# A transformer block on one core: the first projection pass also takes the values' products of four token tiles

## The chip, the core and the metric

The kernel runs on one core of one Trainium2 chip. The metric is the device time of one execution in microseconds, as the median of several runs of the same program. Lower is better.

## The reference, cut to what matters

The kernel computes one block: a gated delta-rule branch (GDN, 4 heads of 128) and a dilated attention branch (8 heads of 64) over the same normed input, an output projection, and a gated feed-forward part, all in float32.

```python
def reference(x, w_in, conv_w, a_log, dt_bias, onorm_g, rel_bias, w_out, g_mix_pre, g_mix_post,
              w_gate, w_up, w_down, g_ffn_pre, g_ffn_post):
    split_at = [int(c) for c in np.cumsum(IN_SIZES)[:-1]]
    for l in range(DEPTH):
        h = rmsnorm(x, g_mix_pre[l])
        proj = h @ w_in[l]
        qa, ka, va, gate_a, beta_a, alpha_a, qb, kb, vb = jnp.split(proj, split_at, axis=-1)
        out_a = gated_deltanet(qa, ka, va, gate_a, beta_a, alpha_a,
                               conv_w[l], a_log[l], dt_bias[l], onorm_g[l])
        out_b = dilated_attention(qb, kb, vb, rel_bias)
        mix = jnp.concatenate([out_a, out_b], axis=-1) @ w_out[l]
        x = x + rmsnorm(mix, g_mix_post[l])
        h = rmsnorm(x, g_ffn_pre[l])
        f = (jax.nn.silu(h @ w_gate[l]) * (h @ w_up[l])) @ w_down[l]
        x = x + rmsnorm(f, g_ffn_post[l])
    return x
```

x is 1024 tokens by 1024 features. Only the start matters here: `h @ w_in`. The row factor of the norm (1 over the root mean square of a token) is put on after the product, so the products can start on x times g alone.

## The kernel before, in words

**Precision.** A float32 product is made of three fp32r products: the left side is split into hi and lo, the right side too, and hi x hi, hi x lo and lo x hi are added in PSUM (`mm3`, line 555). A split takes one instruction on ACT (or DVE) for hi, a cast, and one on DVE (or POOL) for lo.

**Input.** x comes transposed in tiles of one k tile (128 features) by half of the tokens (512): `load_xt` (line 1302) issues the load of `xT`, 256 KB, and `prep_xt` makes `hTh` on ACT and `hTl` on DVE. There are 16 such tiles, eight for each half; six xT buffers. x comes a second time in token tiles (`load_x`, line 1316, 512 KB, three buffers `xn`), from which `norm_in` takes the row factor: a square with a running sum on ACT into `junk`, two small operations on DVE and POOL, `rtok`; for each four tiles four transposes on PE turn it into `rb`, the factor along the tokens.

**Weights.** Chunks of 128 columns of w_in come in two pieces of four k tiles each (`wr`, 256 KB, four buffers). `prep_w` (line 697) splits a piece and fires an event for it.

**The first items.** ORDER (line 57) begins with k0, q0, bv0: GDN's first key and query head, then the first half of the attention values with the eight columns of beta and alpha (264 columns in all, chunks 24 and 25, `wba`). `main` (line 1252) runs, for each half of the tokens, `proj_first` (line 723), which takes k0 and q0 side by side into two PSUM banks `pj` (48 products of 512 columns, a k tile at a time), and then `proj_v` for four token tiles (line 770; 24 products of 264 columns for each tile, into a bank `tp`). I call the two runs of `proj_first` the first and the second pass. There are two `pj` banks and four `tp` banks. A `pj` bank of these passes is emptied by a copy to `raw` on ACT (`raw_sink`, line 1223), which is multiplied by `rb` later; a `tp` bank by two ACT instructions, `vs` (the values, stored to `d_v` by a DMA of 128 KB) and `bp` (beta and alpha).

**What sets the order.** All instructions are issued by a planner (`Weaver`, line 237). Work is written as strands that yield an instruction, a request for a buffer or an event; the planner keeps a clock for each engine, takes the instruction that by its own costs can start first, and among those by priority. So the order on each engine is fixed when the program is built, and each engine runs its instructions in that order. DMAs of this part are issued from SP's queue, also in order; a DMA's issue can wait for a buffer. A request for a buffer is granted when the planner reaches it, without an instruction: who asks first has it.

Of the kernel before, what the change touches and what calls it, by code (L numbers as in the profile page):

```python
# [48 lines left out]
LATE = 2000.0  # L49
PB = 2  # L50
SW = 832

FAR = {2: 256, 3: 576, 4: 448, 5: 416, 6: 256, 7: 576}
PWO = (2, 3, 2)
# [158 lines left out]
class After:  # L213


    def __init__(self, *aps, late=0.0):
        self.aps, self.late = aps, late


class Strand:  # L220
# [16 lines left out]
class Weaver:  # L237
# [125 lines left out]
    def run(self, *until):  # L363
        while not all(e.set for e in until):
# [15 lines left out]
            for s in live:  # L380
                if s.alts is not None:
                    s.req = s.alts[0]
                    if s.ver >= 0:
                        s.req = min(s.alts, key=lambda r: self.finish(s, r, live))
                names = [x.tensor.name for x in s.req.aps] if isinstance(s.req, After) else \
                    [x[0] for op in s.req for x in op.ins + op.outs]
                v = sum(self.ver.get(n, 0) for n in names)
                if v != s.ver:
                    s.ver = v
                    if isinstance(s.req, After):  # L390
                        s.data = max([t for x in s.req.aps for t, _ in self.wr.get(x.tensor.name, {}).values()] + [0.0])
# [12 lines left out]
                first = min(first, s.start)  # L404
# [137 lines left out]
def block_kernel(ctx: ExitStack, tc: tile.TileContext, a, out):  # L542
# [109 lines left out]

    def load_w():

        first = chunks(order[0]) + chunks(order[1])
        got = {c: [] for c in first}
        evs = {c: [Event() for _ in range(2)] for c in first}
        for i in range(2):
            for n, c in enumerate(first):
                wr = yield rawS.get([P, 4, P], F32, name="wr")  # L660
                yield SY.dma_start(wr[:], a["w_in"][c][:, 4 * i:4 * i + 4, :])
                got[c].append(wr)
                evs[c][i].fire()
                if not i:
                    w.spawn(prep_w(c, got[c], evs[c]), 1)
                yield from load_xt(4 * i + n, 0)
                if not i and not n:
                    yield SY.dma_start(gT[:], a["g_mix_pre_t"])
            for k in (2, 3):
                yield from load_xt(4 * i + k, 0)  # L670
        yield SY.dma_start(wba[:], a["w_ba"])
        yield from load_item(order[2])
        yield SY.dma_start(ident[:], a["c_ident"])
        for t in range(4):
            yield from load_x(t)
        for k in range(KT):
            yield from load_xt(k, 1)
        for t in range(4, NT):
            yield from load_x(t)
        ev_x.fire()  # L680
        for item in order[3:]:
            yield from load_item(item)

    def load_item(item):
        for c in chunks(item):
            z, evs = [], [Event() for _ in range(2)]
            for i in range(2):
                wr = yield rawS.get([P, 4, P], F32, name="wr")
                yield SY.dma_start(wr[:], a["w_in"][c][:, 4 * i:4 * i + 4, :])
                z.append(wr)  # L690
                evs[i].fire()
            w.spawn(prep_w(c, z, evs), 1)

    ev_x = Event()
    ev_wh = {(c, i): Event() for c in loaded for i in range(2)}

    def prep_w(c, raw, got):
        hi, lo = [], []
        for i in range(4):
            if c in (24, 25):  # L700
                z = yield wS.get([P, 2, WB], F32R, name="w")
            else:
                z = yield wS.get([P, 4, P], F32R, name="w")
            (lo if i % 2 else hi).append(z)
        wts[c] = hi, lo
        for i, (wh, wl) in enumerate(zip(hi, lo)):
            yield got[i]
# [9 lines left out]
            yield After(wr[:])  # L717
            yield from split_sb(wh, wl, wx)
            rawS.put(wr)
            ev_wh[c, i].fire()  # L720
# [33 lines left out]
    def proj_qk(c0, m, ev):  # L754
# [12 lines left out]
        for hf in range(2):  # L767
            yield from proj_half(c0 + m, hf, sink)

    def proj_v(m, tiles=range(NT)):  # L770
        c0 = 24 + 2 * m
        yield loaded[c0]
        yield loaded[c0 + 1]
        wc = [wts[c0], wts[c0 + 1]]
        n = 256 if m else WB

        def sink(t, ps, bank):
            vs = yield outS.get([P, 4, 64], F32, name="vs")
            yield ev_r[t]
            r = rtok[:, t:t + 1]  # L780
            yield A.activation(vs[:], ps[:, 0:256].rearrange("p (h d) -> p h d", h=4), AF.Copy, scale=r)
            if not m:
                yield A.activation(bp[:, :, t], ps[:, 256:WB], AF.Copy, scale=r)
            (pj if m else pt).put(bank)
            yield SY.dma_start(d_v[t, :, 4 * m:4 * m + 4, :], vs[:])
            outS.put(vs)
            ev_v[m][t].fire()
        for t in tiles:
            if m:
                bank = ps = yield pj.get([P, n], F32, name="pj")  # L790
            else:
                bank = yield pt.get([P, 4, P], F32, name="tp")
                ps = bank[:].rearrange("p k j -> p (k j)")[:, 0:n]
            for k0 in range(0, KT, 2):
                ops = []
                wh, wl = (z[k0 % 4 // 2] for z in wc[k0 // 4])
                for k in (k0, k0 + 1):
                    h, l = (z[:, k % 2, :] if not m else z[:].rearrange("p (k x) c -> p k (x c)", x=2)[:, k % 2, :]
                            for z in (wh, wl))
                    ops += mm3(ps[:], *h_of(k, t * P, P), h, l, k == 0, k == KT - 1)  # L800
                yield ops
                if t == NT - 1:
                    wS.put(wh, wl)
            w.spawn(sink(t, ps, bank), 1)
        if not m and tiles[-1] == NT - 1:
            w.spawn(beta_alpha(ev_v[0]), 2)

# [444 lines left out]
    def main():  # L1252
# [43 lines left out]
    with ExitStack() as s0:  # L1296
# [10 lines left out]
        def prep_xt(k, hf, x):  # L1307
# [5 lines left out]
            px.put(x)  # L1313
            ev_xt[k, hf].fire()

        def load_x(t):
            x = yield px.get([P, D], F32, name="xn", bufs=3)
            yield SY.dma_start(x[:], a["x"][t * P:(t + 1) * P, :])
            done_in.append(w.spawn(norm_in(t, x), 1))

        def norm_in(t, x):
            ss = px.tile([P, 1], F32, name="ss%d" % t)
# [6 lines left out]
            if t % 4 == 3:  # L1329
# [1131 lines left out]
```

## Time and profile before

| | us |
|---|---|
| median of 3 runs | 1217.29 |
| the runs | 1215.97 to 1217.84 |
| the profiled execution's own time | 1217.08 |
| its span, first to last instruction | 1215.3 |
| mean granted TensorE clock | 0.998 of full speed |
| first product on PE starts at | 5.08 |
| second pass starts at | 30.70 |

All times in a profile are counted from the span's start. PE is TensorE's products, PEld its weight loads, DVE VectorE, ACT ScalarE, POOL GpSimd, SP the queue that issues DMAs. The length that the profile gives a product is longer than the distance to the next one, since products overlap in the array; rates are read from starts. Instructions are named out<-in with the kernel's tile names; all of them have the line of the planner's issue, so the names tell them apart.

### The profile page before, as it was taken

The page shows a single profiled execution, that of the slowest core. Times are in us where ns is not written, and L with a number is a line of the kernel's source. Part 1 is how long each engine was busy: PE and PEld are TensorE (multiplying, and loading weights), DVE is VectorE, ACT ScalarE, POOL GpSimd, SP SyncE. Part 2 cuts the span into 40 slices and gives each one's busy share as a digit, 9 for nine tenths or more (in the row PEclk, how much of TensorE's full clock was granted, in tenths as well). Part 3 has the DMA queues.
Part 4 walks back from the last instruction along what each step waited for, and adds up shares of the span by engine and source line. Part 5 has one row for each costly group of instructions (what it writes and reads, how often), then busy time and mean ns, then how long its engine had stood idle before and what let it go on. Part 6 is the DMA issues. An engine that isn't in the chain of part 4 may idle for free.

```text
span 1215.3 us, 19597 instructions
## 1 busy us (share of the span) xinstructions
PE 1198.3 (99%) x7135; PEld 996.0 (82%) x7135; DVE 886.0 (73%) x1633; ACT 544.8 (45%) x1060; POOL 158.0 (13%) x138
## 2 busy tenths in 40 slices
PE   8999999999999999999999999999999999999997
PEld 7888798788888778888788888888888887888886
DVE  4689969646665756676998876787667867876886
ACT  7645622226665654464643333333333344544541
POOL 0143311001111100011101110011100100000111
PEclk9999999999999999999999999999999999999999
DMA  8655363677546355774444433432233238644335
GB/s 279 197 154 164 104 188 102 135 236 239 195 143 204 112 170 181 234 242 163 133 156 139 131 121 122 130 110 70 90 121 122 82 122 312 223 138 149 102 122 207
DMA packets 152359, 192.76 MB, mean 159 GB/s; under 512 B 29976, under 2 KB 77848, under 8 KB 152264
## 3 DMA queue, kind: packets, MB, share of 16 engines
q1 hardware_dynamic: 148040, 189.43, 48.5%
q10 hardware_dynamic: 4224, 2.10, 0.6%
q8 instruction: 56, 0.92, 0.3%
q14 instruction: 39, 0.32, 0.1%
HBM read 135.62 MB, written 59.66 MB: 161 GB/s over the span
## 4 chain that ended last, share of the span: by engine, by line
PE 90%; DVE 4%; DMA 2%; issue 1%; ACT 1%; POOL 1%; SPq 0%; DVEq 0%; POOLq 0%; ACTq 0%
PE bank L286 48%; PE pj L286 22%; PE pw L286 6%; PE tp L286 5%; PE p L286 3%; PE pS L286 2%; PE pV L286 2%; PE pm L286 2%; DVE yc L286 1%; DMA views<-in_w_down 1%; DMA mx<-d_mix 0%; SPq L286 0%; DMA db<-in_w_down 0%; DMA cbv<-d_bv 0%; DVE x L286 0%
## 5 line engine op out<-in xcount | busy, mean ns | idle before, releaser
L286 PE MATMUL pj<-hTh,w 128*128 128x512 f32 x768 | 263.5, 404 | 5.1 <-ACT hTh L286 5.1
L286 PEld LDWEIGHTS pj<-hTh,w 128*128 128x128 f32 x768 | 145.2, 189 | 39.4 <-issue 5.3
L286 ACT CAST wbh<-wraw 128x512 fp32r<-128x512 f32 x130 | 80.4, 621 | 198.6 <-PE bank L286 122.1
L286 PE MATMUL pj<-hTl,w 128*128 128x512 f32 x384 | 151.0, 393 | 0.0
L286 DVE TENSOR_TENSOR wbl<-wraw,wbh 128x512 fp32r<-128x512 f32 x131 | 92.3, 707 | 29.1 <-ACT wbh L286 29.0
L286 PE MATMUL bank<-views 128*128 128x512 f32 (+1 forms) x307 | 85.0, 385 | 0.2 <-ACT views L286 0.2
L286 PEld LDWEIGHTS pj<-hTl,w 128*128 128x128 f32 x384 | 72.9, 190 | 12.5 <-DVE hTl L286 0.7
L286 PE MATMUL bank<-views,dah 128*128 128x512 f32 (+1 forms) x214 | 73.5, 379 | 0.0
L286 PE MATMUL bank<-dbh,views 128*128 128x512 f32 (+1 forms) x201 | 70.3, 380 | 0.0
L286 PEld LDWEIGHTS bank<-views 128*128 128x128 f32 x307 | 57.4, 188 | 12.0 <-ACT views L286 0.7
L286 POOL TENSOR_TENSOR m<-m,m 128x512 f32<-128x512 f32 x18 | 28.0, 1556 | 253.3 <-DVE r L286 153.3
L286 ACT CAST w<-wr 128x512 fp32r<-128x512 f32 x53 | 32.6, 618 | 50.5 <-PE pj L286 43.3
L286 PE MATMUL bank<-dbh,dah 128*128 128x512 f32 (+1 forms) x129 | 49.1, 381 | 0.0
L286 DVE TENSOR_TENSOR w<-wr,w 128x512 fp32r<-128x512 f32 x44 | 30.7, 703 | 23.2 <-ACT w L286 22.0
L286 DVE SCALAR_TENSOR_TENSOR yc<-raw,convw,yc 128x1024 f32<-128x1024 f32 x36 | 46.6, 1294 | 0.5
L286 PEld LDWEIGHTS bank<-views,dah 128*128 128x128 f32 x214 | 40.0, 188 | 7.7
L286 PE MATMUL pw<-woh,mh 128*128 128x512 f32 x112 | 45.2, 404 | 0.0
L286 PE MATMUL pw<-woh,ml 128*128 128x512 f32 x112 | 43.8, 391 | 0.0
L286 PE MATMUL pw<-wol,mh 128*128 128x512 f32 x112 | 43.7, 390 | 0.0
L286 PEld LDWEIGHTS bank<-dbh,views 128*128 128x128 f32 x201 | 37.7, 188 | 7.1
L286 DVE TENSOR_TENSOR m<-bank,m 128x512 f32<-128x512 f32 x44 | 30.1, 686 | 18.1 <-PE bank L286 18.0
L286 ACT ACTIVATE Sr<-Sr,mx 128x384 f32<-128x384 f32 (+3 forms) x64 | 38.2, 597 | 6.4 <-DVE mx L286 5.9
(384 smaller groups left out, 3073.8 us busy)
## 6 DMA issues: line engine op xcount, KB each, us to landing
wr<-in_w_in SPq DMA_DIRECT2D x56, 256.0 KB
wraw<-in_w_gate SPq DMA_DIRECT2D x52, 256.0 KB
wraw<-in_w_up SPq DMA_DIRECT2D x52, 256.0 KB
views<-d_hid SPq DMA_DIRECT2D x47, 256.0 KB
db<-in_w_down SPq DMA_DIRECT2D x40, 256.0 KB
da<-d_hid SPq DMA_DIRECT2D x30, 256.0 KB
d_hid<-x SPq DMA_DIRECT2D x22, 256.0 KB
d_hid<-r SPq DMA_DIRECT2D x22, 256.0 KB
```

The lines of the kernel that those rows point to most:

```text
L286: op.fn(*op.args, **op.kw)
```

## The change

The first pass also takes the values' products of the first four token tiles, two k tiles at a time: after each two k tiles of k0 and q0 stand 24 products of the values into four `tp` banks. The weights of k0 and q0 are loaded and split in pieces of two k tiles (128 KB), with an event for each; the value weights' pieces stand between them on SP's queue, and `gT` and `wba` come early. `After` can wait for a part of a tile. A new strand, `warm`, sets 512 columns of `junk` to zero and then yields ten bf16 products on them in a `tp` bank. The strands of `norm_in` get a slack of SPREAD = 5000: their transposes are held back on PE until their data are 5 us old by the planner's clock, unless nothing else can go. The sink of the values and the list of their products become functions of their own, `v_sink` and `v_ops`.

```diff
     def load_w():
+        yield SY.dma_start(gT[:], a["g_mix_pre_t"])
...
+        for k in range(0, KT, 2):
+            i, j = k // 4, k % 4
             for n, c in enumerate(first):
...
+                yield SY.dma_start(got[c][i][:, j:j + 2, :], a["w_in"][c][:, k:k + 2, :])
+                evs[c][i][j // 2].fire()
...
+                yield from load_xt(k + n, 0)
+            if not k:
+                yield SY.dma_start(wba[:], a["w_ba"])
+            c = vs[i]
+            wr = yield rawS.get([P, 4, P], F32, name="wr")
...
+            yield SY.dma_start(wr[:], a["w_in"][c][:, 2 * j:2 * j + 4, :])
...
     def proj_first(hf, sinks):
...
+        vs = []
+        if not hf:
+            for t in range(4):
+                z = yield pt.get([P, 4, P], F32, name="tp")
+                vs.append(z)
         for k in range(KT):
             for c, z in zip(cs, ps):
-                yield ev_wh[c, k // 4]
+                yield ev_wh[c, k // 2]
...
+            if vs and k % 2:
+                yield ev_wh[24 + k // 4, k % 4 - 1]
+                for t, z in enumerate(vs):
+                    yield v_ops(0, t, v_rows(0, z), k - 1)
+        for t, z in enumerate(vs):
+            w.spawn(v_sink(0, t, v_rows(0, z), z), 1)
...
-            yield from proj_v(0, range(4 * hf, 4 * hf + 4))
+        yield from proj_v(0, range(4, NT))
...
+        def warm():
+            yield V.memset(junk[:, 0:512], 0.0)
+            tp = yield pt.get([P, 4, P], F32, name="tp")
+            yield [mm(tp[:].rearrange("p k j -> p (k j)"), junk[:, 0:P], junk[:, 0:512]) for _ in range(10)]
+            pt.put(tp)
...
-            done_in.append(w.spawn(norm_in(t, x), 1))
+            done_in.append(w.spawn(norm_in(t, x), 1, SPREAD))
...
+        w.spawn(warm(), 0)
```

What the planner makes of it is seen in the order of the built programs, without times. On PE before, at the program's start, with buffer numbers (pj_157 is k0's bank, pj_158 q0's; w_162 and w_173 their hi weights):

```order
L2457 UNCONDITIONAL_BRANCH
L286 MATMUL pj_157<-hTh_104,w_162 128x512
L286 MATMUL pj_157<-hTl_105,w_162 128x512
L286 MATMUL pj_157<-hTh_104,w_163 128x512
L286 MATMUL pj_158<-hTh_104,w_173 128x512
L286 MATMUL pj_158<-hTl_105,w_173 128x512
L286 MATMUL pj_158<-hTh_104,w_174 128x512
```

On PE now, from the ninth product of the program (pj_156 and pj_157 are the two banks, tp_158 the first value tile's, w_187 and w_188 hi and lo of the values' first piece):

```order
L287 MATMUL pj_156<-hTh_104,w_171 128x512
L287 MATMUL pj_157<-hTh_104,w_178 128x512
L287 MATMUL pj_157<-hTl_105,w_178 128x512
L287 MATMUL pj_157<-hTh_104,w_179 128x512
L287 MATMUL tp_158<-w_187,hTh_104 128x264
L287 MATMUL tp_158<-w_188,hTh_104 128x264
L287 MATMUL tp_158<-w_187,hTl_105 128x264
```

The first twelve products are those of before, and behind them stand value products instead of the next k tile. On PE now, where the first pass with its values ends and the second pass begins:

```order
L287 MATMUL tp<-w,hTl 128x264
L287 LDWEIGHTS junk
L287 MATMUL tp<-junk 128x512
...
L287 MATMUL tp<-ident,rtok 128x128 x4
L287 MATMUL pj<-hTh,w 128x512
L287 MATMUL pj<-hTl,w 128x512
```

The ten products on `junk` stand here, each with a weight load, and nowhere else: at the program's start `proj_first` asks for all four `tp` banks before `warm`'s memset is issued. On ACT before, around the copies of the first pass:

```order
L286 CAST w<-wba 128x2x8
L286 COPY raw<-pj 128x512
L286 CAST w<-wr 128x2x256
L286 COPY raw<-pj 128x512
L286 ACTIVATE junk,ss_268<-xn 128x1024
L286 ACTIVATE junk,ss_274<-xn 128x1024
L286 ACTIVATE vs<-tp,rtok 128x256
```

On ACT now, up to the same two copies; four squares into `junk` and four `hTh` of the second half and the first `vs` stand ahead of these rows:

```order
L287 ACTIVATE hTh<-xT,gT 128x512
L287 ACTIVATE bp<-tp,rtok 128x8
L287 ACTIVATE hTh<-xT,gT 128x512
L287 ACTIVATE vs<-tp,rtok 128x256
L287 ACTIVATE hTh<-xT,gT 128x512
L287 ACTIVATE bp<-tp,rtok 128x8
L287 ACTIVATE hTh<-xT,gT 128x512
L287 ACTIVATE vs<-tp,rtok 128x256
L287 ACTIVATE bp<-tp,rtok 128x8
L287 ACTIVATE vs<-tp,rtok 128x256
L287 ACTIVATE bp<-tp,rtok 128x8
L287 COPY raw<-pj 128x512 x2
```

The copies to `raw` have moved from ahead of the evictions of the value tiles, and ahead of the second half's `hTh`, to behind them all. On SP the eight `xT` loads of the second half now follow each other, with the four `d_v` stores behind them; before, two stores stood among them. From the second pass on the order on PE is that of before, apart from buffer numbers.

More of the change, by code (lines that the diff above doesn't have):

```diff
@@ L213, with __init__ @@
 class After:
-    def __init__(self, *aps, late=0.0):
-        self.aps, self.late = aps, late
+    def __init__(self, *aps, late=0.0, part=False):
+        self.aps, self.late, self.part = aps, late, part
 class Strand:
@@ L390, in run @@
                     if isinstance(s.req, After):
-                        s.data = max([t for x in s.req.aps for t, _ in self.wr.get(x.tensor.name, {}).values()] + [0.0])
+                        own = [self.region(x) if s.req.part else (x.tensor.name, -1, -1) for x in s.req.aps]
+                        s.data = max([t for n, q, f in own for (p, g), (t, _) in self.wr.get(n, {}).items() if p & q and f & g] + [0.0])
                     else:
@@ L685, in load_item @@
         for c in chunks(item):
-            z, evs = [], [Event() for _ in range(2)]
+            z, evs = [], [[Event()] for _ in range(2)]
             for i in range(2):
@@ L716, in prep_w @@
                 wh, wl, wx = wh[:], wl[:], wr[:]
-            yield After(wr[:])
-            yield from split_sb(wh, wl, wx)
+            for j, ev in enumerate(got[i]):
+                yield ev
+                x = (slice(None), slice(2 * j, 2 * j + 2) if len(got[i]) > 1 else slice(None))
+                yield After(wx[x], part=len(got[i]) > 1)
+                yield from split_sb(wh[x], wl[x], wx[x])
+                ev_wh[c, 2 * i + j].fire()
             rawS.put(wr)
-            ev_wh[c, i].fire()
         loaded[c].fire()
@@ L768, in proj_qk, with v_rows, v_ops, v_sink @@
             yield from proj_half(c0 + m, hf, sink)
+    def v_rows(m, bank):
+        return bank if m else bank[:].rearrange("p k j -> p (k j)")[:, 0:WB]
+    def v_ops(m, t, ps, k0):
+        c0 = 24 + 2 * m
+        ops = []
+        wh, wl = (z[k0 % 4 // 2] for z in wts[c0 + k0 // 4])
+        for k in (k0, k0 + 1):
+            h, l = (z[:, k % 2, :] if not m else z[:].rearrange("p (k x) c -> p k (x c)", x=2)[:, k % 2, :]
+                    for z in (wh, wl))
+            ops += mm3(ps[:], *h_of(k, t * P, P), h, l, k == 0, k == KT - 1)
+        return ops
+    def v_sink(m, t, ps, bank):
+        vs = yield outS.get([P, 4, 64], F32, name="vs")
+        yield ev_r[t]
+        r = rtok[:, t:t + 1]
+        yield A.activation(vs[:], ps[:, 0:256].rearrange("p (h d) -> p h d", h=4), AF.Copy, scale=r)
+        if not m:
+            yield A.activation(bp[:, :, t], ps[:, 256:WB], AF.Copy, scale=r)
+        (pj if m else pt).put(bank)
+        yield SY.dma_start(d_v[t, :, 4 * m:4 * m + 4, :], vs[:])
+        outS.put(vs)
+        ev_v[m][t].fire()
     def proj_v(m, tiles=range(NT)):
```

64 lines of the change are left out of this document (22 added, 42 removed).

## The prediction

> **What bounds the kernel now.** The page comes first: how full TensorE (PE) is, and how much of the chain that ended last runs on it.
>
> ```profile
> span 1215.3 us, 19597 instructions
> PE 1198.3 (99%) x7135; PEld 996.0 (82%) x7135; DVE 886.0 (73%) x1633; ACT 544.8 (45%) x1060; POOL 158.0 (13%) x138
> PE 90%; DVE 4%; DMA 2%; issue 1%; ACT 1%; POOL 1%; SPq 0%; DVEq 0%; POOLq 0%; ACTq 0%
> ```
>
> PE is busy for 99% of the span and carries 90% of the chain. So a change pays or costs what it takes out of, or puts into, PE's own row of work. Next the chain in order of time (start, length, what), for the first part of the program, which is all that the change touches, and where this stretch of PE pieces ends.
>
> ```profile
> 5.08 13.68 PE pj L286 x48
> 18.77 12.09 PE tp L286 x100
> 30.86 10.89 PE pj L286 x48
> 41.75 12.08 PE tp L286 x100
> 53.83 5.45 PE pj L286 x24
> ...
> 117.45 4.80 PE pj L286 x21
> ```
>
> From 5.08 us on PE pieces follow each other: the first pass (48 products into two pj banks), four token tiles of the values (96 products and four transposes, tp), the second pass, the other four tiles. Between 53.83 and 122.25 (117.45 + 4.80) the chain stays on PE too. So if the second pass starts later by some amount, all that follows starts later by that amount. Where it starts is the whole question. Now PE's timeline at those places (start, length, what, how many; in brackets the idle time before and what ended it):
>
> ```profile
> 5.08 0.79 PE L286 MATMUL pj<-hTh,w 128*128 128x512 f32 x1 [5.08 <-ACT hTh L286]
> 8.75 0.63 PE L286 MATMUL pj<-hTl,w 128*128 128x512 f32 x1
> 9.18 0.97 PE L286 MATMUL pj<-hTh,w 128*128 128x512 f32 x2
> 9.99 0.39 PE L286 MATMUL pj<-hTl,w 128*128 128x512 f32 x1
> ...
> 18.60 0.41 PE L286 MATMUL tp<-w,hTh 128*128 128x264 f32 x2
> ...
> 28.07 0.60 PE L286 MATMUL tp<-ident,rtok 128*128 128x128 f32 x4
> 28.43 0.49 PE L286 MATMUL tp<-w,hTh 128*128 128x264 f32 x2
> ...
> 30.70 0.39 PE L286 MATMUL pj<-hTh,w 128*128 128x512 f32 x1
> ```
>
> Starts count here, not lengths. At 8.75 a product follows its neighbour after 0.43 us: the clock is still low. From 9.99 to 18.60 stand the last 38 of the 48, 0.227 us each. The first ten took 4.91 us, of which 10 x 0.427 = 4.27 is the low clock and 0.64 is waiting for h and weights. The four transposes take 0.36 (28.07 to 28.43), so the 96 value products take 30.70 - 18.60 - 0.36 = 11.74, or 0.122 each.
>
> **The change part by part.** *The products themselves.* The same 48 and 96 products run, two k tiles of the weights and then two of the values in turn. PE starts when the first h tile is ready, as before. Ten of the twelve products of the first pair lie in the low clock again, for the zeros are not ahead of them: in the built order they stand behind the last value product (the last order rows under the change). So the end of this block, T1, is 30.70 - 0.36 = 30.34. Smaller pieces can at best remove the 0.64 of waiting; at worst the first value piece is late. I bound that by the longest wait of PE in the trace, 1.3:
>
> ```profile
> PE tp L286 <- DVE y L286: 1.6, 2, 1.3
> ```
>
> I take 0 within -0.6 and +1.0, for after the first pair data lead. A pair keeps PE for 24 x 0.122 + 12 x 0.227 = 5.7 us, and in five such us the DMA moves more than the 1 MB that a pair needs (two xT of 256 KB, two half and one whole piece of weights); one stage's row, with DVE's busy time as its third count and GB/s last:
>
> ```profile
> 35.00:40.00 5.00, 5.00 (x24) 4.13 (x22) 0.54 (x4) 3.10 (x6) 1.65 (x3) 1.00 0.93 291
> ```
>
> *The zeros.* All four tp banks are held by the values from the start, and the zeros need one; it comes free after the first tile's eviction. Ten products of 512 columns by 0.227 are 2.27 us, then the four transposes 0.36: PE is through at 30.34 + 2.63 = 32.97. The trace has no bf16 row, so the fp32r row of the same shape is taken; the ends are 0.122, as at 264 columns, and 0.43, as at the low clock: PE through at 31.9 or at 35.0.
>
> The Trainium skill (TensorE: Matmul & The Clock Gate, "LDWEIGHTS") prices a load of 128 columns at 128 / 1.2 ns, and ("What overlaps and what doesn't") lets it overlap only where the row group differs; by that the zeros take about 3.2 us and PE is through at 33.9. The rows speak against it: each of the products at 0.227 has its own load.
>
> *ACT's queue is the cost I see.* The second pass needs the two pj banks. Before, ACT copied them out while PE was on the value tiles (18.12). Now that cover is gone: they are copied only behind the four tiles' evictions, and between those evictions stand four of the eight h tiles of the second half. ACT works in its order, as these rows show (start, length, what, idle before and what ended it):
>
> ```profile
> 18.12 0.59 ACT L286 COPY raw<-pj 128x512 f32<-128x512 f32 x1 [1.76 <-PE pj L286]
> ...
> 24.69 0.48 ACT L286 ACTIVATE vs<-tp,rtok 128x256 f32<-128x256 f32 x1 [1.18 <-PE tp L286]
> ...
> 26.69 1.38 ACT L286 ACTIVATE hTh<-xT,gT 128x512 fp32r<-128x512 f32 x2 [0.49 <-DMA xT<-in_x_t]
> 27.98 0.26 ACT L286 ACTIVATE bp<-tp,rtok 128x8 f32<-128x8 f32 x1
> ...
> 30.50 1.34 ACT L286 ACTIVATE hTh<-xT,gT 128x512 fp32r<-128x512 f32 x2
> 31.74 0.26 ACT L286 ACTIVATE bp<-tp,rtok 128x8 f32<-128x8 f32 x1
> 31.89 0.47 ACT L286 ACTIVATE vs<-tp,rtok 128x256 f32<-128x256 f32 x1
> 32.25 0.28 ACT L286 ACTIVATE bp<-tp,rtok 128x8 f32<-128x8 f32 x1
> 32.40 0.73 ACT L286 ACTIVATE hTh<-xT,gT 128x512 fp32r<-128x512 f32 x1
> 33.36 0.73 ACT L286 ACTIVATE hTh<-xT,gT 128x512 fp32r<-128x512 f32 x1 [0.23 <-DMA xT<-in_x_t]
> ```
>
> The bp at 27.98 belongs to the same bank as the vs at 24.69: its data were there, and it stood over 2 us behind an h tile that waited for its DMA. Steps, start to start: vs 0.36 (31.89 to 32.25), bp 0.15, h tile 0.62 (two from 30.50 to 31.74), the copy 0.59 to its end.
>
> The first tile's products end three tiles (18 x 0.122 = 2.20) ahead of T1; vs comes 0.22 later, as at 24.69 (tile two's last product starts at 18.60 + 48 x 0.122 = 24.47): 28.36. From there four vs (1.44), four bp (0.60), four h tiles (2.48) and the first copy (0.59) end at 33.47. With 0.05 to PE's start (the h tile that ended at 5.03 released PE at 5.08 in the first rows: 4.31 + 0.72) the second pass starts at **33.5 at the earliest, +2.8**.
>
> That holds if every h tile's DMA is there. The last one's was late before: 33.36, after a wait. If it lands as before, ACT has behind it 0.62, two vs and two bp (1.02), the copy 0.59, and 0.05: 35.64, **+4.9**. SP's queue decides:
>
> ```profile
> 13.47 7.65 SPq L286 DMA_DIRECT2D xn<-in_x  x4
> 21.16 0.91 SPq L286 DMA_DIRECT2D xT<-in_x_t  x2
> 22.34 0.33 SPq L286 DMA_DIRECT2D d_v<-vs  x1
> 22.71 2.79 SPq L286 DMA_DIRECT2D xT<-in_x_t  x4
> 25.59 0.38 SPq L286 DMA_DIRECT2D d_v<-vs  x1
> 28.23 0.99 SPq L286 DMA_DIRECT2D xT<-in_x_t  x2
> ...
> xT<-in_x_t SPq DMA_DIRECT2D x16, 256.0 KB
> d_v<-vs SPq DMA_DIRECT2D x16, 128.0 KB
> ```
>
> The fourth xn waits for ACT's first square before and after, which still comes behind the weights' last casts, so I leave the xT loads' start where it is. Two stores of d_v that stood among them now stand behind. Seven loads after the first and two half-sized stores took 33.36 - 26.69 = 6.67 us, 0.83 a load; without the stores the last h tile starts at 32.53 and the second pass at 34.8: **+4.1**. I take this, as the row nearest to it is the same loads' own, and keep 2.8 and 4.9 as ends.
>
> *Edits at nothing.* Eight casts of 256 columns instead of four of 512, gT first, wba early, the junk memset: ACT and DVE do them while PE has the block's 25 us. Both raw products by rb now on DVE (POOL had one): by the stage's row above DVE is busy there for 0.54 of 5 us, and the projections that need them start only with what follows the second pass. From the second pass on PE's order is the same to the end, apart from buffer numbers.
>
> **Sum.** The profiled execution took 1217.08 (span 1215.3, 1.8 around it), 0.21 under the median 1217.29 of the runs. 1217.08 + 4.1 = 1221.2; the median to be expected is 1221.4.
>
> **The rivals.**
> 1. *The zeros decide, not ACT* (not slower by what can be told). If ACT is through before 32.97, PE goes on there: +2.3, 1219.6. It needs the eighth h tile started by 30.7 and half a microsecond off ACT's row; or the 0.64 of waits go and every load is early (33.5 - 0.64 = 32.9, +2.2). For it: ACT's steps were taken from few rows. Against it: 33.36. Chance 0.11.
> 2. *The zeros run first, as the words say.* Then ten products save 0.2 each, and the waits go: T1 = 27.7. Even then ACT's row ends 3.16 after T1 at best: 30.9, +0.2, 1217.5. Against it: the built order. Chance 0.02. The Trainium skill (TensorE: Matmul & The Clock Gate, "What's actually happening") says that about 3.4 us of activity of any kind opens the clock gate, which would save the 2.0; the rows show the change some 4.5 us after PE's start.
> 3. *The clock falls in the gap.* PE would stand about 1.8 us in two pieces between T1 and 34.8 (4.46, less 2.27 and 0.36). If the clock falls, the second pass pays 10 x 0.2 again: 1223.4. Against it: waits of 1.3 left it up. Chance 0.08.
> 4. *The delay is swallowed later.* At 122.3 the chain leaves PE for DVE and others. If that part hangs on something the second pass does not feed, up to 4.1 vanish: down to 1217.3. It needs work there that was waiting for no projection, and the rows show none. Chance 0.05.
>
> **How the numbers follow.** The forecast has 0.74. A measurement of this kernel can tell about 0.2%, 2.4 us, from no change. Slower: 0.74 + 0.08 + 0.01 of rival 4 = 0.83. Within: rival 1's 0.11, 0.01 of rival 2, 0.02 of rival 4 = 0.14. Faster: the rest of rivals 2 and 4, 0.03. The range: below, 2.8 less 0.64 plus the 0.21 on 1217.08, 1219.4, and 0.2 for the runs' spread: 1219.2; above, rival 3's 1223.4, which also takes in 4.9 with up to 1.0 for a late first value piece.
>
> **What would show it.** Right: the first PE row at about 5.1, the last value product near 30.3, junk products behind it and not ahead, then a wait of pj for ACT raw, the second pass at 33.5 to 35.6, and the later stages shifted by the same amount. Wrong: junk rows ahead of the first h; a second pass by 33.0 with no wait for ACT; the low clock after it; or a shift at 53.8 that is smaller by 122.

## The result and the profile after

| | before | after |
|---|---|---|
| median, runs of this comparison (6 each) | 1216.94 us | 1223.95 us |
| the runs | 1215.97 to 1217.84 | 1221.46 to 1225.17 |
| ratio, 95% interval | | 1.0054 (1.0044 to 1.0065) |
| the profiled execution | 1217.08 us (span 1215.3) | 1223.33 us (span 1221.2) |

The change makes the kernel slower by 7.0 us, where 4.1 was forecast, and the median lies 0.55 above the upper end of the range. The page of after, first the lines that answer to those of before:

```profile
span 1221.2 us, 19638 instructions
PE 1201.0 (98%) x7144; PEld 996.5 (82%) x7145; DVE 888.0 (73%) x1640; ACT 544.2 (45%) x1062; POOL 157.6 (13%) x138
PE 84%; DVE 5%; DMA 5%; ACT 2%; issue 2%; SPq 1%; POOL 1%; DVEq 0%; POOLq 0%; ACTq 0%
```

PE works 2.7 us longer (2.3 of it the zeros), the span grows by 5.9, and PE's share of the chain that ended last falls from 90% to 84%: more than half of what was added is waiting. Of the 6.25 us by which the two profiled executions differ, 0.35 lies outside the span: 1.8 us of an execution lie there before (1.7 to 1.9 in all runs of before beside the experiments), 2.1 to 2.8 in the six runs of after. PE's timeline of after (start, length, what, how many; in brackets the idle time before and what ended it) shows where it begins:

```profile
5.15 0.79 PE L287 MATMUL pj<-hTh,w 128*128 128x512 f32 x1 [5.15 <-ACT hTh L287]
...
29.68 0.28 PE L287 MATMUL tp<-w,hTl 128*128 128x264 f32 x1
30.89 2.32 PE L287 MATMUL tp<-junk 128*128 128x512 bf16 x9 [0.93 <-ACT bp L287]
33.05 0.60 PE L287 MATMUL tp<-ident,rtok 128*128 128x128 f32 x4
35.15 0.50 PE L287 MATMUL pj<-hTh,w 128*128 128x512 f32 x1 [1.50 <-ACT raw L287]
```

The last value product starts at 29.68. The zeros wait 0.93 for a tp bank, take 2.16 (30.89 to 33.05; one of the ten records is missing), the transposes follow, and then PE stands for 1.50 until ACT has copied a pj bank to raw. The second pass starts at 35.15 where before had 30.70: +4.45. ACT's timeline of the same stretch shows why the copy is late:

```profile
32.31 0.27 ACT L287 ACTIVATE bp<-tp,rtok 128x8 f32<-128x8 f32 x1
32.85 0.72 ACT L287 ACTIVATE hTh<-xT,gT 128x512 fp32r<-128x512 f32 x1 [0.27 <-DMA xT<-in_x_t]
33.48 0.46 ACT L287 ACTIVATE vs<-tp,rtok 128x256 f32<-128x256 f32 x1
33.84 0.27 ACT L287 ACTIVATE bp<-tp,rtok 128x8 f32<-128x8 f32 x1
33.99 0.47 ACT L287 ACTIVATE vs<-tp,rtok 128x256 f32<-128x256 f32 x1
34.34 0.28 ACT L287 ACTIVATE bp<-tp,rtok 128x8 f32<-128x8 f32 x1
34.49 1.09 ACT L287 COPY raw<-pj 128x512 f32<-128x512 f32 x2
```

Both copies stand behind all evictions and h tiles, and the last h tile waits for its load until 32.85. The same row of work was there before, but the copy at 18.12 stood ahead of it. The zeros alone would have held PE to 33.4 (33.05 and 0.36 for the transposes), so in this execution ACT's row adds the last 1.7 of the 4.45.

So the second pass is 4.45 late, of 5.9 in the span. The rest is lost far behind the change. By the starts of the same PE instructions in both traces, after stands 4.60 behind before from 54 to 390 us, 4.83 when the output projection (pw) begins, 6.9 at its end, and 6.13 at the end of the program. The chain of waits over the output projection, first of before (495 to 575 us), then of after (500 to 575 us), by engine and line in shares:

```profile
by line: PE pw L286 77.3%; PE tp L286 7.4%; DMA mx<-d_mix 7.1%; SPq L286 2.0%; PE rp L286 2.0%; POOL n_r L286 1.3%; DVE y L286 1.0%; DVE mx L286 0.9%; issue 0.6%; DVE mh L286 0.5%; PE rt L286 0.1%; DVE n_m L286 0.1%; DVE ss L286 0.1%; DVEq 
```

```profile
by line: DMA gt<-d_gt 15.2%; PE pw L287 14.4%; issue 10.7%; DMA d_h<-h2s 8.7%; DMA x<-in_x 6.6%; DVE y L287 6.5%; DMA mx<-d_mix 4.8%; ACT junk L287 4.8%; SPq L287 4.3%; POOL n_r L287 3.6%; DVE x L287 3.5%; DVE mx L287 2.9%; PE tp L287 2.0%;
```

Before, PE's own products are 77% of this stretch of the chain; in after's profiled execution they are 14%, and transfers on SP's queue and the norm on DVE carry most of the rest. The forecast had no term for that, so the experiments ask two things: what holds the second pass, and whether this second loss belongs to the change.

### The profile page after: what moved, and what is told of

It reads as the page before. It is cut to its first block, busy times and chain, and to the rows that moved or that the text cites. A ratio compares the mean times of both kernels' runs of the same rounds, so it can differ in the third digit from the quotient of the medians.

```text
span 1221.2 us, 19638 instructions
## 1 busy us (share of the span) xinstructions
PE 1201.0 (98%) x7144; PEld 996.5 (82%) x7145; DVE 888.0 (73%) x1640; ACT 544.2 (45%) x1062; POOL 157.6 (13%) x138
## 4 chain that ended last, share of the span: by engine, by line
PE 84%; DVE 5%; DMA 5%; ACT 2%; issue 2%; SPq 1%; POOL 1%; DVEq 0%; POOLq 0%; ACTq 0%
PE bank L287 48%; PE pj L287 20%; PE tp L287 4%; PE p L287 3%; PE pw L287 3%; PE pS L287 2%; PE pV L287 2%; PE pm L287 2%; SPq L287 1%; DMA gt<-d_gt 1%; DVE yc L287 1%; DMA xT<-in_x_t 1%; DVE x L287 1%; DMA d_h<-h2s 1%; DVE y L287 1%
## 5 line engine op out<-in xcount | busy, mean ns | idle before, releaser
L287 ACT CAST w<-wr 128x512 fp32r<-128x512 f32 (+1 forms) x55 | 32.2, 586 | 53.6 <-PE pj L287 44.1
L287 DVE TENSOR_TENSOR w<-wr,w 128x512 fp32r<-128x512 f32 (+1 forms) x48 | 31.2, 656 | 21.0 <-ACT w L287 17.9
```

The lines of the kernel that those rows point to most:

```text
L287: op.fn(*op.args, **op.kw)
```

## The experiments

The first four ran on one chip (before there: 1218.31 median of 19 runs), the next three on another (1218.01, 17 runs), the last four on a third (1217.82, 19 runs). Theory A is the prediction's: ACT's row holds the second pass.

### Without the zeros

```diff
-        w.spawn(warm(), 0)
```

> The changed kernel without the ten products on junk; everything else as in the change. Theory A (ACT's queue holds the second pass: its two pj banks are copied out behind the value tiles' evictions and behind h tiles that wait for DMAs): taking the products away gains nothing, since the second pass (35.15 us in the changed kernel) waits for the copies; in this build a square that waits for the fifth xn also stands ahead of the copies, so it starts at 36 to 37.5 and the time is 1224 to 1226, no better than the changed kernel's 1223.95. Rival B (the ten misplaced products are the loss, 2.2 us of PE and 0.9 of waiting for their bank): the second pass starts near 32 and the time falls by 2 to 3, to 1221 to 1222.

Measured: 1225.21 us, ratio 1.0055 (1.0041 to 1.0068). PE, and then windows of PE's clock (columns: window, length, then busy time and count of PE, PEld, DVE, ACT and POOL, the granted clock, the DMA share and GB/s):

```profile
31.66 0.62 PE L287 MATMUL tp<-ident,rtok 128*128 128x128 f32 x4 [1.75 <-issue]
39.48 0.80 PE L287 MATMUL pj<-hTh,w 128*128 128x512 f32 x1 [7.20 <-ACT raw L287]
```

```profile
35.00:40.00 5.00, 0.52 (x1) 0.50 (x2) 1.44 (x3) 3.52 (x11) 0.55 (x1) 0.50 0.88 292
40.00:45.00 5.00, 5.00 (x17) 3.98 (x16) 1.22 (x5) 3.27 (x6) 1.53 (x3) 0.71 0.94 322
```

Taking the zeros out buys nothing: PE waits 7.20 us instead of 1.50, for the same copy. It came later than the 36 to 37.5 expected: the fifth square, which I had counted, waited 1.49 us for its xn, and the last h tile of the second half came at 34.41, against 32.85 in after. So theory A holds, B falls; the time lies in the expected range though the start does not. The rows also show what the long wait does: the granted clock falls to 0.50 and the second pass starts slowly; in after, whose wait is 1.5, it does not.

### The zeros first

```diff
         def warm():
-            yield V.memset(junk[:, 0:512], 0.0)
             tp = yield pt.get([P, 4, P], F32, name="tp")
+            yield V.memset(junk[:, 0:512], 0.0)
```

> The changed kernel with the bank for the ten products asked for ahead of the memset, so that they stand first on PE, as the change says. Theory A: the clock is up early and the first pass with its values ends 2 to 2.5 us sooner (near 27.5 instead of 29.96), but ACT's order has now all eight h tiles of the second half and three squares ahead of the copies to raw; the second pass starts at 38 to 40.5, and the time is 1227 to 1230, slower than the changed kernel. Rival B (the misplaced products are the loss): the second pass starts at 28 and the time is 1215 to 1217.

Measured: 1228.5 us, ratio 1.0084 (1.0070 to 1.0098). PE's start:

```profile
1.25 4.45 PE L287 MATMUL tp<-junk 128*128 128x512 bf16 x10 [1.25 <-DVE mhalf L287]
5.59 0.79 PE L287 MATMUL pj<-hTh,w 128*128 128x512 f32 x1
...
6.97 0.71 PE L287 MATMUL pj<-hTh,w 128*128 128x512 f32 x2
7.52 0.40 PE L287 MATMUL pj<-hTl,w 128*128 128x512 f32 x1
...
40.76 0.79 PE L287 MATMUL pj<-hTh,w 128*128 128x512 f32 x1 [6.60 <-ACT raw L287]
```

Now the zeros do what the change's words say, and it helps little. They run at the low clock themselves and hold the first real product until 5.59, and the clock rises only near 7.1. The last value product starts at 29.52, against 29.68 in after: 0.16 gained, where I expected over 2. The wait for raw is 6.60, and the clock falls in it again. The second pass starts a little behind the expected 38 to 40.5; the time lies in the expected range.

### The copies first

```diff
+            if k == KT - 1:
+                evs = [w.spawn(sink(hf, z), 1) for sink, z in zip(sinks, ps)]
             if vs and k % 2:
...
-        return [w.spawn(sink(hf, z), 1) for sink, z in zip(sinks, ps)]
+        return evs
```

The sinks of the two pj banks are spawned right behind the pass's last products, ahead of the last value products.

> The changed kernel with the copies to raw spawned right after the last product of the first pass, ahead of the last value products; the planner then puts them between the h tiles, ahead of the evictions, and the ten products fall inside the second pass. Theory A: the second pass starts where the values end, at 30.0 to 30.6; the ten products still cost 2.2 of PE later, so from the k1 projection on the delay against before is 1.5 to 2.3 instead of 4.6, and the time 1219 to 1221. Rival B: the products cost what they cost in the changed kernel, and the time stays within 1 us of 1223.95.

Measured: 1217.37 us, ratio 0.9989 (0.9979 to 0.9999). The second pass starts at 30.91 without any wait for raw; the zeros stand inside it:

```profile
30.91 0.39 PE L287 MATMUL pj<-hTh,w 128*128 128x512 f32 x1
...
40.01 2.33 PE L287 MATMUL tp<-junk 128*128 128x512 bf16 x9
```

So the place of two ACT instructions is what held the start of the second pass. It is not the whole first loss: the zeros are now paid inside the second pass, and at the end of the values this kernel stands 3.1 us behind before's profile, where after stands 4.6 behind. The time is 1.6 to 3.6 us better than I expected for another reason: up to the output projection the planner wrote a different order for PE, and in that stretch this kernel takes back 2.5 (table below). So its time alone does not price the copies.

### The copies first, without zeros

Both edits above.

> Both edits: copies to raw early, no products on junk. Theory A: nothing is left that delays the second pass; it starts at 30.0 to 30.6, a few tenths ahead of before (30.70), and the time is 1216.0 to 1218.5, where the upper part is for the stage near 511 to 562 us, in which the changed kernel lost another 2.0 us with the same order on PE. If that later loss comes from the new order at the start by itself, 1218.5 to 1219.5; if it comes with the delay, or is chance of the run, it is gone or differs from run to run.

Measured: 1214.98 us, ratio 0.9972 (0.9963 to 0.9982): faster than before, and 1 us under the expected 1216.0 to 1218.5. The copies now stand between the h tiles:

```profile
28.39 0.57 ACT L287 COPY raw<-pj 128x512 f32<-128x512 f32 x1
29.39 1.38 ACT L287 ACTIVATE hTh<-xT,gT 128x512 fp32r<-128x512 f32 x2 [0.43 <-DMA xT<-in_x_t]
30.67 0.57 ACT L287 COPY raw<-pj 128x512 f32<-128x512 f32 x1
```

The second pass starts at 30.94, not ahead of before's 30.70 as expected, but without a wait. The values end 0.7 behind before's profile, the first pw comes 0.7 ahead of it; between them the planner set some of PE's products in another order, so the gain over before is not the start's.

### A delay and nothing else

```diff
                 wh, wl = wts[c]
+                if hf and not k and c == cs[0]:
+                    extra = [mm(z[:], wh[0][:, 0, :], next(iter(h_of(0, 512, 512))), True, True) for _ in range(20)]
+                    for x in extra:
+                        x.cost = 0.0
+                    yield extra
```

This is the kernel before, with a pure delay on PE and every engine's order as it was.

> The kernel before, with 20 more products of 512 columns on PE ahead of the second pass (hTh by w into k0's bank, each starting the sum anew, so the result is unchanged); the planner counts them at nothing, so every engine's order is that of before. 20 x 0.227 = 4.54 us. Theory D (a delay of the second pass is carried one to one, and what the changed kernel lost later was its own): the second pass proper starts at 30.70 + 4.54 = 35.24, k1 at 58.2, the stretch of the output projection's products (first to last) keeps its 97.9 us, and the time is before + 4.5. Rival E (the delay itself lets the norm stage around 511 to 562 us lose more, since its DMAs meet others): the same start, but that stretch takes about 100 us and the time is before + 6.5 to 7. Rival F (the delay is partly swallowed): below before + 3.5.

Measured: 1223.22 us, ratio 1.0045 (1.0032 to 1.0058), +5.2.

```profile
6.33 0.79 PE L286 MATMUL pj<-hTh,w 128*128 128x512 f32 x1 [6.33 <-ACT hTh L286]
...
33.05 4.93 PE L286 MATMUL pj<-hTh,w 128*128 128x512 f32 x21
37.82 0.39 PE L286 MATMUL pj<-hTl,w 128*128 128x512 f32 x1
```

The 20 products add 4.54, this execution also had its first h tile 1.2 later than the profile of before, and its clock rose 2.0 us later behind the first product. Behind the delay the kernel stands 6.89 behind that profile up to 510 us, without a change, and 7.59 at the end. So PE's pieces do carry a delay one to one for 450 us (rival F falls), and the output projection adds a little: it takes 98.5, between D's 97.9 and E's 100, and the time lies between theirs too.

### The changed kernel again

No edit.

> The changed kernel, unchanged. Theory D1 (the 2 us that its profiled execution lost between 511 and 562 us are that execution's own): first product of the output projection again at before + 4.8 (481.6), but the stretch from its first to its last product 98 us as in the other kernels (97.6 to 99.3) and not 99.96, and the median nearer to before + 4.5 to 5.5. Rival D2 (they belong to the program): the stretch takes 99.5 to 100.5 us again and the median is before + 6.5 to 7.

Measured: 1223.07 us (6 runs, 1221.39 to 1223.96), ratio 1.0039 (1.0027 to 1.0052), +5.1. PE at the start, and the chain from 500 to 582 us:

```profile
31.14 2.32 PE L287 MATMUL tp<-junk 128*128 128x512 bf16 x10 [0.54 <-ACT bp L287]
33.29 0.60 PE L287 MATMUL tp<-ident,rtok 128*128 128x128 f32 x4
35.90 0.50 PE L287 MATMUL pj<-hTh,w 128*128 128x512 f32 x1 [2.01 <-ACT raw L287]
```

```profile
by line: PE pw L287 75.7%; DMA mx<-d_mix 8.0%; PE tp L287 7.2%; PE rp L287 2.2%; SPq L287 2.0%; POOL n_r L287 1.2%; DVE y L287 0.9%; PE bank L287 0.8%; DVE mx L287 0.8%; issue 0.6%; DVE mh L287 0.5%; PE rt L287 0.1%; DVE n_m L287 0.1%; DVE 
```

The start repeats: wait for a bank, zeros, wait for raw. The chain in the output projection does not: it is PE's for 76% here, where the first execution of this very program had 14%. Its length of 98.8 and the +5.1 both lie within the bounds of D1. So more than half of the second loss was one execution's; 0.9 of it comes back.

### Zeros first and copies first

Both edits, after the diffs above.

> Both edits at once: the ten bf16 products run ahead of the first h tile (their bank is taken before the value tiles take theirs), and the copies of the two pj banks are put on ACT right behind the first pass's last products, ahead of the last value products. Theory A (ACT's queue holds the second pass, not the clock): no wait of pj for ACT raw, second pass at 30.5 to 31.0, time 1214 to 1217, as without the zeros. Rival B (the zeros are worth what ten products at the low clock cost): first pass 1.5 to 2 us shorter, second pass by 29.5, 1213 or less.

Measured: 1221.34 us, ratio 1.0027 (1.0016 to 1.0037): slower, against both theories.

```profile
30.34 0.50 PE L287 MATMUL pj<-hTh,w 128*128 128x512 f32 x1 [0.79 <-ACT raw L287]
...
32.25 0.50 PE L287 MATMUL pj<-hTh,w 128*128 128x512 f32 x1 [0.95 <-ACT raw L287]
```

The planner puts the copies behind five and two h tiles, so PE waits for raw twice, 1.7 in all. That does not make 3.3 us. The profiled execution took 1218.84 at a clock of 0.998; the runs from 1221.3 to 1223.7 show 0.995 to 0.997, which suggests that the clock was low for longer somewhere in them; this trace does not show it, and where stays open.

### Other banks for the first pass

```diff
-            z = yield pj.get([P, 512], F32, name="pj")
+            z = yield (pj if hf else pm).get([P, 512], F32, name="pj" if hf else "pm")
...
                 yield A.copy(z, ps[:])
-                pj.put(ps)
+                (pj if hf else pm).put(ps)
```

Here ACT's order up to the copies is left alone and what makes PE wait is taken away. Farther on, between about 80 and 160 us, the planner set some of PE's products in another order.

> The changed kernel, but the first pass takes its two banks from the pool pm, which is idle there, and the second pass takes the two pj banks: nothing waits for the copies to raw, and on ACT the evictions, the h tiles and the copies stand in the changed kernel's order. Theory A (the wait for the copies behind ACT's row is one term, the zeros with their bank's eviction are the other): no wait of pj for ACT raw; the zeros still start at about 30.9 behind the first bp, PE is through with them and the transposes at 33.4 to 33.7, and the second pass starts there, +2.7 to +3.0 on before; time before + 3 to 4. Rival B (the second pass waits for its own h tiles or data on that stretch): the second pass still starts at 34.5 or later.

Measured: 1218.21 us, ratio 1.0006 (0.9997 to 1.0015). No wait for raw, though ACT copies the banks only at 35.89:

```profile
30.77 0.39 PE L287 MATMUL pj<-hTh,w 128*128 128x512 f32 x1
...
32.16 2.33 PE L287 MATMUL tp<-junk 128*128 128x512 bf16 x10
...
34.69 0.48 PE L287 MATMUL pj<-hTh,w 128*128 128x512 f32 x1
```

```profile
35.89 1.09 ACT L287 COPY raw<-pm 128x512 f32<-128x512 f32 x2
```

Six products of the second pass run ahead of the zeros, so the zeros no longer wait for their bank either; what is left is 34.69 - 32.16 = 2.53 for zeros and transposes. Behind them the trace stands 2.7 behind before's, as expected; the median, +0.4, is better than the 3 to 4 expected. The profiled execution (1220.16) was the longest of its 11 runs, and against before's profile it lost 2.0 us in the output projection.

### Other banks, without zeros

Both edits: the banks as above, and `w.spawn(warm(), 0)` left out.

> The same, without the strand of the zeros. Theory A: nothing stands between the last value product and the second pass, which starts at 29.8 to 30.6 (before: 30.70), and the time is before -1 to +1. Rival B: as above, a wait for an h tile.

Measured: 1214.55 us (1213.74 to 1215.56), ratio 0.9974 (0.9964 to 0.9984). This is below both kernels, and level with the copies first without zeros (0.9972). Its page, and the second pass on PE's timeline:

```profile
span 1212.7 us, 19617 instructions
PE 95%; DVE 2%; DMA 1%; ACT 1%; issue 1%; POOL 0%; SPq 0%; DVEq 0%; POOLq 0%; ACTq 0%
```

```profile
30.00 0.39 PE L287 MATMUL pj<-hTh,w 128*128 128x512 f32 x1
```

The second pass starts at 30.00 right behind the last value product, and PE has 95% of the chain. It beats the expected -1 to +1, and the start is not why: the values end 0.25 ahead of before's profile, the first pw comes 1.0 ahead (again with some of PE's products in another order), and 1.5 more are gained near 1024 us, where PE waits in the profile of before and not here.

### The kernel before, executed twice more

> The kernel before, unchanged: what the stretch of the output projection and the steps from the first to the last product of PE take from one execution to the next. Theory D1 (such stretches vary by a microsecond or two by themselves): first to last product of the output projection 98 to 100 us in one of these looks, where the profile of before had 97.9. Rival D2 (before is steady there): 97.5 to 98.2 in both.

> The kernel before, unchanged, a second look. Theory D1: the stretch from the first to the last product of the output projection is 98 to 100 us in this look or in the other. Rival D2: 97.5 to 98.2 in both.

Measured: 1217.13 and 1216.62 us. The output projection took 97.5 and 97.4, so D1 falls, and D2 holds to a tenth. What neither theory was about is the start. The second pass of each of the two executions:

```profile
31.99 0.39 PE L286 MATMUL pj<-hTh,w 128*128 128x512 f32 x1
```

```profile
32.33 0.39 PE L286 MATMUL pj<-hTh,w 128*128 128x512 f32 x1
```

Against 30.70 in the profile of before these are 1.3 and 1.6 late, and yet both executions are as fast at the end. The starts of PE's products, from the traces (us; "values end" is the last value product of the second four tiles, pw the output projection; the last two columns are lengths):

| | second pass | values end | first pw | last pw | last product | pw's length | from there to the end |
|---|---|---|---|---|---|---|---|
| before | 30.70 | 53.55 | 476.74 | 574.65 | 1207.83 | 97.9 | 633.2 |
| before, 2nd execution | 31.99 | 54.84 | 477.98 | 575.50 | 1207.89 | 97.5 | 632.4 |
| before, 3rd execution | 32.33 | 55.19 | 478.55 | 575.95 | 1207.38 | 97.4 | 631.4 |
| after | 35.15 | 58.15 | 481.57 | 581.53 | 1213.95 | 100.0 | 632.4 |
| after again | 35.90 | 58.88 | 482.32 | 581.11 | 1214.59 | 98.8 | 633.5 |
| a delay alone | 37.6 | 60.44 | 483.63 | 582.15 | 1215.41 | 98.5 | 633.3 |
| other banks | 30.77 | 56.30 | 479.33 | 579.23 | 1211.16 | 99.9 | 631.9 |
| other banks, no zeros | 30.00 | 53.30 | 475.73 | 573.52 | 1205.52 | 97.8 | 632.0 |
| copies first | 30.91 | 56.64 | 477.35 | 574.91 | 1206.67 | 97.6 | 631.8 |
| copies first, no zeros | 30.94 | 54.25 | 476.07 | 573.89 | 1206.89 | 97.8 | 633.0 |
| no zeros | 39.48 | 64.06 | 487.27 | 585.41 | 1217.67 | 98.1 | 632.3 |
| zeros first | 40.76 | 65.59 | 488.61 | 587.95 | 1219.83 | 99.3 | 631.9 |
| zeros and copies first | 30.34 | 54.98 | 476.33 | 575.36 | 1207.79 | 99.0 | 632.4 |

(For the delay alone the second pass proper is put at 33.05 + 4.54.) The means of the three traces of before and the two of after differ by 3.85 at the second pass, 3.99 at the end of the values, 4.19 at the first pw, 5.95 at the last pw and 6.57 at the last product.

## Why the prediction was right or wrong, by its steps

**Sign, cause and place: right.** ACT's row held the second pass, by a wait of PE for raw, and other banks or an earlier copy take that wait away (30.77 and 30.91). Both put the time within 0.15% of before. By the traces the zeros then still cost their part, as rival 1 said: the values end 2.75 and 3.09 behind before's profile, where after's end 4.60 and 5.33 behind. Only without the wait and without the zeros is the loss gone there (0.25 ahead and 0.70 behind).

**T1.** Forecast 30.34 (within -0.6 and +1.0); the last value product ended its slot at about 29.8 and 30.4 in the two executions. Data led after the first pair, as taken.

**The zeros.** Forecast 10 x 0.227 behind T1. They took 2.16 and 2.15, so 0.216 each: bf16 at this shape costs nearly what fp32r does. By an estimate from the Trainium skill (TensorE: Matmul & The Clock Gate, "LDWEIGHTS") their loads would have made it about 3.2 us; the trace disagrees, and the loads were hidden. What I had left out is the wait of 0.93 and 0.54 for a bank's bp ahead of them. It costs nothing in after, for ACT's copy is later still (PE is through at 33.4 and 33.7, the second pass starts at 35.15 and 35.90).

**ACT's row.** Forecast: last h tile at 32.53, second pass at 34.8, the bounds 33.5 and 35.64. Measured: 32.85 and 33.61, so 35.15 and 35.90. The mechanism is the one named, a load of xT that lands late; the stores of d_v did leave its way, but against before's 33.36 the last load gained 0.51 instead of the 0.83 that I took off for them, and in the second execution nothing.

**What it is worth against before.** Here I compared with one trace, whose start happened to be early: 30.70, where the two further executions have 31.99 and 32.33. Against the mean of the three the shift is 3.85, so the term of 4.1 was near by two errors that cancel, and that is luck.

**The step that failed is the sum: that "all that follows starts later by that amount".** It does to the first pw (3.99 at the end of the values, then 4.19), and it does in the delay alone (6.89 from 54 to 510 us). In the output projection 1.8 more is lost on the mean (5.95), and 0.6 behind it. By traces that is 6.6 instead of 4.1, and about 0.4 more lies outside the span, which the sum kept at 1.8 us. By medians it is +7.0 and +5.1 in the two sets of runs; the interval of the second (1.0027 to 1.0052) takes in the forecast, and its median of 1223.07 lies within the range. So the size of the miss, though not its sign, differs from one set of runs to the next.

What PE does in the output projection is seen ahead of the transposes of y, the result of the norm. First of before, then of after, then of after again:

```profile
508.21 0.69 DVE L286 TENSOR_TENSOR mx<-mx,rp 128x512 f32<-128x512 f32 x1 [1.49 <-DMA mx<-d_mix]
511.34 0.66 PE L286 MATMUL tp<-ident,y 128*128 128x128 f32 x4 [0.34 <-DVE y L286]
```

```profile
513.69 0.69 DVE L287 TENSOR_TENSOR mx<-mx,rp 128x512 f32<-128x512 f32 x1 [2.14 <-DMA mx<-d_mix]
516.81 0.66 PE L287 MATMUL tp<-ident,y 128*128 128x128 f32 x4 [0.98 <-DVE y L287]
541.39 0.63 PE L287 MATMUL tp<-ident,y 128*128 128x128 f32 x4 [0.22 <-DVE y L287]
556.43 0.63 PE L287 MATMUL tp<-ident,y 128*128 128x128 f32 x4 [0.50 <-DVE y L287]
```

```profile
514.70 0.69 DVE L287 TENSOR_TENSOR mx<-mx,rp 128x512 f32<-128x512 f32 x1 [2.40 <-DMA mx<-d_mix]
517.82 0.66 PE L287 MATMUL tp<-ident,y 128*128 128x128 f32 x4 [1.24 <-DVE y L287]
```

So the second loss of this stage is PE waiting for y: in the rows up to the last pw 0.34 us before, 1.70 in after, 1.24 in after again. By the starts of the same products, the steps to these transposes are longer than the shortest in any trace by 0.50, 2.46 and 1.40 in all; with the 97.4 to 97.5 of the two executions without such a wait that gives, to a tenth, the lengths in the table, 97.9, 100.0 and 98.8. At the first of these waits DVE in turn stands for one load, mx, and PE's wait grows by what DVE's does (0.64 and 0.90 against 0.65 and 0.91). The load was issued 25.7 us after the first pw in all three. The sign of it was on view before the change: the one row of waits that the prediction shows, PE for y, counts this wait and one behind the stage. I used it to bound another term, read the chain only to 122 us and took the rest as PE's.

What makes y late is not settled. The delay of the second pass alone does not decide it: at the first of the waits the kernel with zeros and copies first, 0.4 ahead of before's profile, waits 1.25, and the one without zeros, 10.5 behind it, does not wait. The second and third execution of before do not wait there either. Nor does PE's share of the chain tell the loss: over 500 to 575 us it is 76% before, 14% in after and 75% in after again, but 15% without zeros, with a length of only 98.1, and 75% with zeros and copies first, with 99.0.

**The rivals.** Rival 1 (the zeros decide) was wrong for after, but is what happens with other banks, at 2.5 us of trace. Rival 2 (zeros first) was wrong, and its price too: run first, they end the block 0.16 sooner than in after, not 2.6. Rival 3 (the clock falls in the gap): not in the two traces of after, with waits of 1.5 and 2.0 us, but it does around the waits of 6.6 and 7.2. Rival 4 (swallowed later) is wrong for the shift as a whole; but the two further executions of before make up for 1.3 and 1.6 us behind the first pw, at 511, 588 and 1024 us, where the profile of before has PE waiting for y, views or dal. At 1024 us after and after again gain 0.9 and 1.5 on that profile in the same way.

## What to carry to other kernels

When work of one engine is pulled together, look for the short instruction on another engine that frees its buffers, and give it its place in that engine's row, or other buffers; here two copies of half a microsecond, set behind the rest, held PE until 35.15. Ask too what would hold PE next: with other banks the zeros and the transposes behind them still took 2.5. Do not carry a shift along the chain of PE past a stage in which PE already waits a little for another engine: look there for PE's own waits, and price a microsecond or two of loss. And take more than one execution of the kernel before, for a start that varies by 1.6 us is a good part of the 4.1 to be forecast.

## What the runs showed of the hardware

**When the clock rises** is much less fixed than one trace shows. Reading the spacing of the first products (0.43 at the low clock, 0.23 at the full one), the change came 3.7 us after the first product in after, 4.8 in before, 5.1 in after again, 5.6 and 7.0 in the two further executions of before; and some 6 us after the first zero when the zeros ran first. So part of any difference between two traces at the second pass is this. Two rows of the third execution of before, the first still at the low clock, the second no longer:

```profile
11.46 0.96 PE L286 MATMUL pj<-hTh,w 128*128 128x512 f32 x2
12.26 0.40 PE L286 MATMUL pj<-hTl,w 128*128 128x512 f32 x1
```

The Trainium skill (TensorE: Matmul & The Clock Gate, "What's actually happening") gives a free-running window of about 3.4 us, with a scatter of half a microsecond about it and 6 to 14 slow products; the 8 to 13 slow products here agree, the scatter is over 3 us.

**When it falls:** no sign of it behind waits of 1.5 and 2.0 us in after. Without the zeros the granted clock is 1.00 from 30 to 32.5 us, 0.69 from 32.5 to 33.0 and 0.50 behind. So it fell within 0.8 us of the start of the wait of 7.2 (31.66 + 0.62 = 32.28), and about 3 us behind the last value product (29.62), with a wait of 1.75 and four transposes between. The Trainium skill (TensorE: Matmul & The Clock Gate, "What's actually happening") puts the limit at one idle window of about 3.4 us; here the clock fell though no single wait had lasted that long, and how little work in a window lets it fall is not placed by these runs.

**Zeros to warm up** cost their own time at the low clock: ten took 4.34 (1.25 to 5.59), and they held the first real product back by 0.4.
